# Hybrid gMLP and SSD block on one core: a hand-written order from the last wide pair to the second projection, PSUM banks from a queue, and operands of the second projection made beside the first

## The chip, the cores and the metric

The kernel runs on one core of one Trainium2 chip. Its time is the device time of one execution in microseconds (us); several executions are timed and the median counts. The profile comes from one further execution, whose own time is given beside its span. All data are fp32. A core has a matrix engine (TensorE, PE in the profile, with its weight loads as PEld), a vector engine (VectorE, DVE), a scalar engine (ScalarE, ACT), GpSimd (POOL), and a SyncE (SP) that only issues DMAs here. TensorE writes its sums into PSUM, eight banks of 128 x 512 fp32.

## The reference, cut to what matters

One layer with sequence 1024 and model width 1024, followed by a norm:

```python
h = rms_norm(x, norm_w) * (1 + scale) + shift          # scale, shift, gate from c @ ada_w
gm_u, gm_v, gm_z, ssm_z, xbc, dt_raw, g_a, g_b = split(h @ w_in)
y_a = spatial_gating(gelu(gm_u), gelu(gm_v), ...) * silu(gm_z)
xbc = silu(causal_depthwise_conv(xbc, conv_w, conv_b))
xs, bm, cm = split(xbc);  dt = softplus(dt_raw + dt_bias)
y_b = ssd_scan(xs, dt, -exp(a_log), bm, cm) + xs * d_skip   # 32 heads, 8 groups, chunks of 128
y_b = grouped_rms_norm(y_b * silu(ssm_z), ssm_norm_w)       # 2048 wide
merged = sigmoid(g_a) * (y_a @ w_proj_a) + sigmoid(g_b) * (y_b @ w_proj_b)
return rms_norm(x + gate * (merged @ w_out), final_norm_w)
```

## The kernel before, in words

**Products.** Each fp32 operand is split into a high part in fp32r (a rounded copy) and a low part (the operand less its high part), and a product is three matmuls: high by high, high by low, low by high. The three large products use a Strassen scheme with seven block products p1 to p7. Splitting one operand is two instructions: a cast for the high part (on ACT) and a subtraction for the low part (on DVE).

**Stages, in order.**
1. The input projection, in "pairs" of 128 columns (`pair`, `product` L567 to L573). Each of a pair's seven products takes twelve 128x512 matmuls. The last pair is called g14: it makes gate columns, and its sums c1 and c2 go through tanh (L906) and are stored to `th_d`. It runs its products as p1, p5, p6, p3, p7, p2, p4 and calls `beside(n)` (L1240) after each of the first five sums is copied out.
2. The SSD scan, in 32 steps (8 groups by 4 double chunks, listed in `order`, L1155). For each step, `decay_rows` and `decay_exps` make exponentials (ea, dcy) on ACT, with a mask on POOL between; `prep_products` makes transposes and products of B and C into banks px and pc, and weights them on DVE (dcy, xd); `prep_b` and `prep_xe` copy the rest out (bn, xe). `front` then makes yi and the state product sp; `back` makes yn and the step's output. The order of these is written by hand in the loop at L1388 to L1409.
3. Between the steps the first projection, `y_a @ w_proj_a`, is drawn as filler (`proj_a`, L1312, called through `draw`): 192 draws of two matmuls. It runs over eight column blocks dd; each has two PSUM banks pma and, per block, a high and a low part of the weights (wah, wal), made after the second and the fourth k step of the block before. When a block is complete, DVE multiplies its banks with a gate (tha, L1337), and the result is stored to `mt_d`. Its other operands, ya, are loaded in `beside` and split in `ya_operand` (L1208).
4. The second projection, `y_b @ w_proj_b`, in 56 units: seven products p1, p2, p5, p3, p6, p7, p4 by eight k steps, each unit with twelve matmuls into four banks (`multiply`, L1520). p1, p6, p7 and p4 use the four x banks, p2, p5 and p3 the four y banks. `loads(u)` (L1473) issues the DMAs of a unit, six units ahead; `operands(u)` (L1487) normalizes yn with the row factors rb (L1466), and makes high and low parts (bh, bl at L1505 and L1506; a at L1510 and L1511), four units ahead. After p1 ACT copies the x banks out as c11, and after p2 DVE adds the y banks to it (L1637). Later units make the gated sum (`merged`, L1559 to L1565).
5. The output projection and the last norm.

**What sets the order.** Engines run their instructions in order. A scheduler decides that order from modelled times and priorities, except for instructions that are pinned to program order: all matmuls of these stages, all loads on SP, and whatever goes through `keep` or `pin`. While `hand[0]` is true, every instruction of DVE, ACT and POOL is pinned. It is true only from the first `front` to the end of the SSD steps; the lines of instructions issued in that time show as L56. Stage 4 comes after that: its operands run at the scheduler's choice, but for the first four units, whose high and low parts are pinned.

**Memory.** PSUM banks of the SSD steps come from one ring (`bank`, tag "bk", eight buffers): a new tile waits until the tile eight before it is done. The banks of stage 4 are other tags ("bx0" and so on) in a new pool, which lie on banks that the old tiles held. SBUF slots of 128x512 come from a list `room`, with rings (`ring`, `turn`) for operands that rotate: rb has four slots, bh and bl five each.

Of the kernel before, what the change touches and what calls it, by code (L numbers as in the profile page):

```python
# [35 lines left out]
def hybrid_kernel(  # L36
# [105 lines left out]
    hp = hpool.__enter__()  # L142
    BN = ("b11", "t1", "t2", "b22", "t3", "b21", "t4")
# [337 lines left out]

    def bank(name):

        return psum.tile([P, 512], F32, name=name, tag="bk", bufs=n_banks[0])
# [90 lines left out]
    pending, n_banks = [], [6]  # L575
# [370 lines left out]
    class Group:  # L946
# [72 lines left out]
        def prep_b(self, s):  # L1019
            self.bn[s] = bn = p2x.tile([P, 256], F32, name=f"bn{self.g}_{s}", tag="bn", bufs=3)  # L1020
            A.copy(bn, self.raw[s][1][:, 256:512])  # L1021

        def prep_xe(self, s):
            self.xs[s].append(self.weighted(s, "xe", dde))

# [13 lines left out]
        def front(self, s):  # L1039

            g, nm = self.g, f"{self.g}_{s}"
            sl, dcy, ea = self.pre[s]
            bn, (xd, xe) = self.bn[s], self.xs[s]
            yi = bank(f"yi{nm}")
            for i in range(2):
                for h in range(HPG):
                    j, hh = h // 2, h % 2
                    mm(yi[hh * HD : (hh + 1) * HD, j * 256 + i * P : j * 256 + (i + 1) * P],
                       xd[:, i * 256 + h * HD : i * 256 + (h + 1) * HD], dcy[:, h, i, :])
            sp = bank(f"sp{nm}")  # L1050
# [16 lines left out]
            if not last:  # L1067
                self.nxt = self.state(f"st{nm}_1"), sp
                self.decayed(self.nxt[0], s, 1)

        def back(self, s):
# [16 lines left out]
            G.tensor_add(y1[:, :, t0:], y1[:, :, t0:], m[:, :, t0:])  # L1088
            if self.nxt is not None:
                self.st, sp = self.nxt  # L1090
                V.tensor_add(self.st, self.st, sp[:, 256:512])
                self.nxt = self.state(f"st{nm}_2")
                self.decayed(self.nxt, s + 1, 0)
# [4 lines left out]
        def post(self, q):  # L1098

            g = self.g  # L1100
            yz = self.yz[q]

            def leave():
                for j in range(2):
                    store(yb_d[2 * g + j][:, q * 512 : (q + 1) * 512], yz[:, j])

            if g < NG - 2 or q == 0:
                later(3, leave)
                later(9, self.squares, yz, [yz[:, j] for j in range(2)])
                later(17, self.post2, q, yz[:, 0])  # L1110
            else:
                later(1, leave)
                sq = [turn(r, f"sq{g}", F32) for r in (y1_r, ym_r)]
                later(1, self.squares, yz, sq, pin)
                later(9, self.post2, q, sq[0])
# [13 lines left out]
        def post2b(self, q, pq):  # L1129
            g = self.g  # L1130
            V.tensor_scalar(ssq[:, g * NCH + q * 4 : g * NCH + q * 4 + 4], pq[:, 0:4], 1.0 / 256, EPS,
                            op0=ALU.mult, op1=ALU.add)
            if q == 1:
# [5 lines left out]
        def post3(self, at_once=False):  # L1139
# [5 lines left out]
            V.tensor_copy(row, pr[0:NCH, 0:P])  # L1145
            to = rs_d[g].rearrange("o (c p) -> (o c) p", p=P)
# [61 lines left out]
    def ya_operand(k):  # L1208
        yh, yl = ya_raw[k]
        for i in range(2):  # L1210
            pin(A.copy(yh[i], f32(yl[i])))
# [13 lines left out]
    def wa_block(dd):  # L1225
        wa_high(dd)
        wa_low(dd)

    def wa_high(dd):
        was[dd] = []  # L1230
        for i, wr in enumerate(war[dd]):
            wh, wl = turn(wah_r[0], f"wah{dd}_{i}"), turn(wal_r[0], f"wal{dd}_{i}")
            A.copy(wh, wr)
# [6 lines left out]
    def beside(n):  # L1240

        if n == 0:
            ya_load(0)
            ya_load(1)
        elif n == 1:
# [16 lines left out]
    held, seconds, fold = [], [], []  # L1262
# [7 lines left out]
    for n, (name, _, _, d1, d2, g) in enumerate(todo):  # L1270
# [32 lines left out]
        if n + 1 == len(todo):  # L1303
            pair(name, ops, lambda t: held.append((d1, t)), lambda t: held.append((d2, t)), beside, True)
# [7 lines left out]
    def proj_a():  # L1312

        for dd in range(KT):
# [20 lines left out]
            keep = pin if dd == KT - 1 else lambda i: i  # L1335
            for h in range(2):
                keep(V.scalar_tensor_tensor(ths[h], ths[h], 1.0, pms[h], op0=ALU.add, op1=ALU.mult))  # L1337
            for h in range(2):
                to = mt_d[dd][:, h * 512 : (h + 1) * 512]
                if hand[0]:  # L1340
                    later(1, store, to, ths[h])
                else:
                    keep(A.dma_start(to, ths[h]))
# [44 lines left out]
    hand[0] = True  # L1388
# [21 lines left out]
    while tasks:  # L1410
        draw(2)
        run_tasks()
    hand[0] = False

    room.extend(ea_r[0] + [st_tag])
    room.extend(tag for k in range(KT - 2) for tag in ya_tags[k])
    draw(left[0] - 5)

    def banks(name, c):
        return [psb.tile([P, 512], F32, name=f"{name}{j}", tag=f"b{c}{j}") for j in range(4)]  # L1420
# [30 lines left out]
    first, rest = room[:3], room[10:21]  # L1451
    del room[10:21], room[:3]
    rb_r, bh_r, bl_r = (([first[n]] + [rest.pop(0) for _ in range(c)], [0]) for n, c in enumerate((3, 4, 4)))
# [127 lines left out]
    room.extend(tag for k in (KT - 2, KT - 1) for tag in ya_tags[k])  # L1581
    for tags, _ in (war_r[0], wah_r[0], wal_r[0], tha_r, y1_r, ym_r):
# [3 lines left out]
    psb = ps3.__enter__()  # L1586
    wo, wor = {}, {}
# [14 lines left out]
    sums, more = [], []  # L1602
    for u, (nm, k) in enumerate(units):
# [10 lines left out]
        multiply(u, ps)  # L1614
        ahead(u)
# [11 lines left out]
        if k % 2 and more and nm not in ("p2", "p5"):  # L1627
            merged(*more.pop(0))
        if k == KT - 1:
            for j in range(4):  # L1630
                with tc.high_priority():
                    if nm == "p1":
                        t = slot_tile(f"c11_{j}")
                        A.copy(t, psx[j])
                        more.append((j, 0, t, f"c11_{j}"))
                    elif nm == "p2":
                        V.tensor_add(more[j][2], more[j][2], psy[j])  # L1637
                    elif nm in ("p5", "p3"):
# [131 lines left out]
```

## Time and profile before

| what | us |
|---|---|
| median of the runs | 1423.65 |
| lowest and highest of three | 1422.61, 1425.19 |
| profiled execution | 1426.2 |
| its span, first to last instruction | 1424.5 |

The mean granted clock of TensorE in the profiled execution is 0.996 of full speed. In the profile's rows, times are in us from the span's start. A timeline row gives the start, the duration (of the whole group where several instructions are joined, with x and their number), engine, line, operation and tiles, and in brackets the time in which the engine was idle before it, with the engine and the line that ended this idleness. A row of the waits gives the engine and what it waited for: total us, how often, and the longest. A row of the windows gives the busy time of each engine in a stretch, the granted clock of TensorE, the busy share of the DMA engines, and GB/s.

### The profile page before, as it was taken

The page shows a single profiled execution, that of the slowest core. Times are in us where ns is not written, and L with a number is a line of the kernel's source. Part 1 is how long each engine was busy: PE and PEld are TensorE (multiplying, and loading weights), DVE is VectorE, ACT ScalarE, POOL GpSimd, SP SyncE. Part 2 cuts the span into 40 slices and gives each one's busy share as a digit, 9 for nine tenths or more (in the row PEclk, how much of TensorE's full clock was granted, in tenths as well). Part 3 has the DMA queues.
Part 4 walks back from the last instruction along what each step waited for, and adds up shares of the span by engine and source line. Part 5 has one row for each costly group of instructions (what it writes and reads, how often), then busy time and mean ns, then how long its engine had stood idle before and what let it go on. Part 6 is the DMA issues. An engine that isn't in the chain of part 4 may idle for free.

```text
span 1424.5 us, 20475 instructions
## 1 busy us (share of the span) xinstructions
PE 1391.4 (98%) x7087; PEld 1152.5 (81%) x7087; DVE 1026.6 (72%) x1821; ACT 783.4 (55%) x1444; POOL 205.2 (14%) x190
## 2 busy tenths in 40 slices
PE   8999999999999999999999999989999989999997
PEld 7678888888888888888887788878888878787886
DVE  4686677776677888788778786377778866948443
ACT  5664575666566665545565554657667633334201
POOL 0000000000000000000010100027879840000000
PEclk9999999999999999999999999999999999999999
DMA  8552333333323687587686764688888767977331
GB/s 264 157 170 83 125 106 110 100 115 104 117 83 112 196 240 220 157 255 225 197 244 187 227 200 133 228 319 280 278 286 286 255 209 259 380 253 292 136 118 74
DMA packets 260524, 277.08 MB, mean 195 GB/s; under 512 B 13596, under 2 KB 210628, under 8 KB 260420
## 3 DMA queue, kind: packets, MB, share of 16 engines
q1 hardware_dynamic: 179396, 195.37, 43.3%
q10 hardware_dynamic: 81024, 80.40, 16.2%
q8 instruction: 56, 0.92, 0.3%
q14 instruction: 48, 0.39, 0.1%
HBM read 191.40 MB, written 84.31 MB: 194 GB/s over the span
## 4 chain that ended last, share of the span: by engine, by line
PE 80%; DMA 6%; DVE 4%; ACT 3%; issue 3%; POOL 3%; SPq 1%; POOLq 0%; ACTq 0%; DVEq 0%
PE xx L571 6%; PE xuz L571 6%; PE xcb L571 6%; PE po L90 6%; PE xz L571 6%; PE x L1527 6%; PE xg L571 3%; PE pma L90 3%; PE yuz L571 3%; PE yx L571 3%; PE yp L1527 3%; PE xv L571 3%; PE ycb L571 3%; PE yz L571 3%; PE yv L571 2%
## 5 line engine op out<-in xcount | busy, mean ns | idle before, releaser
L782 POOL TENSOR_TENSOR wog<-wog,gb 128x1024 f32<-128x1024 f32 x8 | 22.6, 2825 | 725.5 <-ACT wbb L799 530.3
L56 ACT ACTIVATE dcy<-dcy,nacs 128x128 f32<-128x128 f32 x224 | 68.6, 388 | 32.6 <-POOL dcy L56 13.6
L90 PE MATMUL pma<-yh,wah 128*128 128x512 f32 x128 | 43.4, 419 | 1.8 <-ACT bn L1021 1.8
L894 ACT ACTIVATE ac<-ac 128x1024 f32<-128x1024 f32 x32 | 34.0, 1061 | 19.7 <-DVE ac L892 19.6
L1733 ACT ACTIVATE xr<-r 128x1024 f32<-128x1024 f32 x7 | 7.4, 1061 | 66.1 <-issue 39.0
L90 PE MATMUL pma<-yh,wal 128*128 128x512 f32 x128 | 42.8, 415 | 0.0
L56 DVE TENSOR_TENSOR ym<-yn,ea 128x512 f32<-128x512 f32 (+1 forms) x32 | 19.9, 623 | 30.5 <-PE yn L90 30.3
L56 POOL TENSOR_TENSOR yz<-y,sl 128x512 f32<-128x512 f32 x32 | 41.1, 1285 | 0.6
L90 PE MATMUL pma<-yl,wah 128*128 128x512 f32 x128 | 39.9, 393 | 0.0
L90 PE MATMUL yi<-dcy,xd 128*64 128x128 f32 x512 | 35.9, 283 | 3.5 <-DVE xe L1015 2.5
L56 POOL TENSOR_TENSOR y<-y,ym 128x512 f32<-128x512 f32 (+1 forms) x32 | 36.6, 1143 | 17.1 <-DVE ym L56 16.5
L1723 POOL TENSOR_TENSOR r<-r,fnw 128x256 f32<-128x256 f32 (+1 forms) x3 | 2.7, 915 | 247.9 <-ACT xr L1722 247.9
L892 DVE SCALAR_TENSOR_TENSOR ac<-c2x,cwt,ac 128x1023 f32<-128x1023 f32 (+2 forms) x24 | 31.9, 1330 | 9.0 <-ACT ac L890 7.1
L56 DVE TENSOR_TENSOR dcy<-dcy,pc 128x1024 f32<-128x1024 f32 x30 | 36.6, 1219 | 2.4 <-PE pc L93 1.4
L1732 DVE TENSOR_TENSOR r<-po,xr 128x1024 f32<-128x1024 f32 x7 | 8.6, 1225 | 39.8 <-PE po L90 39.7
L1466 DVE SCALAR_TENSOR_TENSOR yn<-yn,par,rb 128x512 f32<-128x512 f32 x32 | 24.9, 779 | 15.7 <-DMA yn<-yb_d 15.7
L56 ACT ACTIVATE ea<-dcy 64x512 f32<-64x512 f32 x56 | 35.3, 630 | 1.5 <-DMA dcy<-acs_d 1.1
L892 DVE SCALAR_TENSOR_TENSOR ac<-c2cb,cwt,ac 128x1023 f32<-128x1023 f32 (+2 forms) x24 | 30.6, 1276 | 7.1 <-ACT ac L890 7.0
L56 POOL TENSOR_SCALAR_AFFINE_SELECT dcy<-dcy 128x1024 f32<-128x1024 f32 x28 | 32.2, 1152 | 19.7 <-ACT ea L56 19.6
L90 PEld LDWEIGHTS yi<-dcy,xd 128*64 128x64 f32 x512 | 28.1, 139 | 7.8 <-issue 5.5
L90 PE MATMUL sp<-xe,bn 128*128 128x256 f32 x112 | 33.4, 415 | 0.0
L56 DVE SCALAR_TENSOR_TENSOR y<-sl,dskt,yi 128x256 f32<-128x256 f32 x64 | 27.7, 473 | 6.3 <-PE yi L90 2.8
(2844 smaller groups left out, 4425.8 us busy)
## 6 DMA issues: line engine op xcount, KB each, us to landing
sl<-s_d SPq DMA_DIRECT2D x32, 768.0 KB
s_d<-ac ACTq DMA_DIRECT2D x32, 512.0 KB
dcy<-acs_d SPq DMA_DIRECT2D x32, 512.0 KB
aw<-in_ada_w_dram SPq DMA_DIRECT2D x16, 512.0 KB
wbr<-in_w_proj_b_dram SPq DMA_DIRECT2D x64, 128.0 KB
wb_d<-wbb ACTq DMA_DIRECT2D x32, 256.0 KB
wb_d<-wbc ACTq DMA_DIRECT2D x32, 256.0 KB
yb_d<-yz ACTq DMA_DIRECT2D x32, 256.0 KB
```

The lines of the kernel that those rows point to most:

```text
L56: return lambda *a, **k: tc.keep_in_program_order(f(*a, **k))
L90: pin(PE.matmul(acc, l, r, start=first, stop=last))
L571: pin(PE.matmul(ps, lw[:, k * P : (k + 1) * P], r[k], start=first and n + k == 0, stop=n == 2 and k == 3, skip_group_check=not first))
L782: G.tensor_mul(w, w, gb)
L892: V.scalar_tensor_tensor(ac[:, s:], cc[:, : S - s], conv_wt[:, 3 - s, i : i + 1], ac[:, s:], op0=ALU.mult, op1=ALU.add)
L894: A.activation(ac, ac, AF.Silu)
L1466: V.scalar_tensor_tensor(t, t, snw[:, n : n + 1], rbs[n // 2, h], op0=ALU.mult, op1=ALU.mult)
L1527: pin(PE.matmul(ps[j], a[:, v, js], r, start=first and n + k == 0, stop=n == 2 and k == KT - 1, skip_group_check=not first))
L1723: G.tensor_mul(r[:, cs], r[:, cs], fnw[:, cs])
L1732: V.tensor_add(r, pw, xr)
L1733: A.activation(xr, r, AF.Square, accum_out=sq[:, 0:1])
```

## The change

- **Order.** `hand[0]` becomes true before the last pair and stays true until the end of p5 (unit 23), so that in this stretch DVE, ACT and POOL run in program order.
- **Last pair.** `beside` now also issues `decay_rows` and `decay_exps` of the first two SSD steps and, after p6's copy, the first two ya operands and the first weight block, with their high parts on DVE (four ya and two wah copies). The other ya operands follow later. The two steps' `prep` and the pair's own last tanh and store come in program order around p2 and p4, where before these were held back or scheduled.
- **PSUM.** A queue `free` holds the numbers of the eight banks, at first in the order 1, 4, 3, 0, 2, 7, 5, 6. A new tile takes the bank at the head of the queue; `release` puts a bank at the end of it behind the instruction that reads it last. The x banks of stage 4 are the first four of the queue at the end of the SSD steps, the y banks the last four.
- **First operands of stage 4.** The first loads and operands are issued in the loop that draws the last filler, at fixed draws, not after it. Each unit's parts (norm, bh, bl, a) follow one another. Rings for these now use slots of the SSD steps: rb three, bh and bl four each. ya slots are handed back one by one as the last block of the first projection consumes them.
- **p1 to p5.** c11's copies and additions are issued directly after p1's and p2's last unit, ahead of the next unit's operands. The last block's store goes through `store`.

The diff, cut to its core:

```diff
+    free, at_bank = [], {}
     def bank(name):
-        return psum.tile([P, 512], F32, name=name, tag="bk", bufs=n_banks[0])
+        if not free and not at_bank:
+            return psum.tile([P, 512], F32, name=name, tag="bk", bufs=6)
+        at_bank[name] = free.pop(0)
+        return psum.tile([P, 512], F32, name=name, tag=f"k{at_bank[name]}")
+    def release(*names):
+        free.extend(at_bank.pop(name) for name in names if name in at_bank)
...
     def start_ssd():
         fetch(2)
-        for n in range(2):
-            later(3 + 5 * n, decays, n + 1)
-            g, s = order[n]
-            later(13 + n, groups[g].prep, s)
+        done_d[0] = 2
...
     def beside(n):
+        first = [(groups[g], i) for g, i in order[:2]]
         if n == 0:
             ya_load(0)
             ya_load(1)
+            first[0][0].decay_rows(first[0][1])
         elif n == 1:
...
+            first[1][0].decay_rows(first[1][1])
+            first[0][0].decay_exps(first[0][1])
         elif n < 5:
             ya_load(2 * n - 2)
             ya_load(2 * n - 1)
-        if n == 4:
-            for k in range(2):
-                ya_operand(k)
-            wa_block(0)
-            for k in range(2, 6):
-                ya_operand(k)
+        if n == 2:
+            ya_operand(0, V.tensor_copy)
+            first[1][0].decay_exps(first[1][1])
+            ya_operand(1, V.tensor_copy)
+            wa_high(0, V.tensor_copy)
+            wa_low(0)
+        elif n == 4:
+            ya_operand(2)
+            ya_operand(3)
+        elif n > 4:
+            first[n - 5][0].prep(first[n - 5][1])
+            ya_operand(n - 1)
...
-            pair(name, ops, lambda t: held.append((d1, t)), lambda t: held.append((d2, t)), beside, True)
+            hand[0] = True
+            pair(name, ops, with_last(5, d1), with_last(6, d2), beside, True)
...
             for h in range(2):
-                keep(V.scalar_tensor_tensor(ths[h], ths[h], 1.0, pms[h], op0=ALU.add, op1=ALU.mult))
+                V.scalar_tensor_tensor(ths[h], ths[h], 1.0, pms[h], op0=ALU.add, op1=ALU.mult)
+                release(f"pma{dd}_{h}")
...
-    n_banks[0] = 8
+    numbered(psum, "k")
+    free.extend(BANKS)
     for k in (6, 7):
         ya_operand(k)
-    decays(3)
-    for f, t in held:
-        f(t)
     decays(4)
...
-    while tasks:
-        draw(2)
-        run_tasks()
-    hand[0] = False
...
-    rb_r, bh_r, bl_r = (([first[n]] + [rest.pop(0) for _ in range(c)], [0]) for n, c in enumerate((3, 4, 4)))
+    rb_r = ea_r[0], [0]
+    bh_r, bl_r = ((r[0][0][:2] + ya_tags[0][2 * n : 2 * n + 2], [0]) for n, r in enumerate((wah_r, wal_r)))
...
-    for u in range(LOAD):
-        loads(u)
-        if u > 1:
-            operands(u - 2)
+    for u in range(3):
+        loads(u)
+    n = 0
+    while tasks:
+        draw(2)
+        run_tasks()
+        ya_free()
+        n += 1
+        if n in (2, 4, 6, 8):
+            operands(n // 2 - 1)
+        if n in (4, 5, 6):
+            loads(n - 1)
     draw(left[0] + 1)
...
+    places_of = {"x": free[:4], "y": free[4:]}
...
+    def emptied_banks(nm):
+        for j in range(4):
+            if nm == "p1":
+                t = slot_tile(f"c11_{j}")
+                A.copy(t, psx[j])
+                more.append((j, 0, t, f"c11_{j}"))
+            else:
+                V.tensor_add(more[j][2], more[j][2], psy[j])
...
         multiply(u, ps)
+        if u < 16 and k == KT - 1:
+            emptied_banks(nm)
         ahead(u)
...
+        if u == 23:
+            hand[0] = False
```

More of the change, by code (lines that the diff above doesn't have):

```diff
@@ L1066, in front @@
             self.nxt = None
-            if not last:
+            release(f"yi{nm}")
+            if last:
+                release(f"sp{nm}")
+            else:
                 self.nxt = self.state(f"st{nm}_1"), sp
@@ L1206, in ya_load, with ya_operand @@
         ya_raw[k] = yh, yl
-    def ya_operand(k):
+    def ya_operand(k, copy=None):
         yh, yl = ya_raw[k]
         for i in range(2):
-            pin(A.copy(yh[i], f32(yl[i])))
+            pin((copy or A.copy)(yh[i], f32(yl[i])))
             pin(V.tensor_sub(yl[i], f32(yl[i]), f32(yh[i])))
@@ L1386, in of @@
         getattr(groups[g], f)(s)
-    hand[0] = True
     draw(6)
@@ L1574, in ahead, with ya_free @@
             operands(u + LEAD)
-    for u in range(LOAD):
-        loads(u)
-        if u > 1:
-            operands(u - 2)
+    emptied = [1]
+    def ya_free():
+        while emptied[0] < KT and left[0] <= 3 * (KT - 1 - emptied[0]):
+            room.extend(ya_tags[emptied[0]])
+            emptied[0] += 1
+    for u in range(3):
+        loads(u)
+    n = 0
[8 more added lines that the diff above has]
+            loads(n - 1)
     draw(left[0] + 1)
-    room.extend(tag for k in (KT - 2, KT - 1) for tag in ya_tags[k])
-    for tags, _ in (war_r[0], wah_r[0], wal_r[0], tha_r, y1_r, ym_r):
+    ya_free()
+    for tags in (war_r[0][0][:2], wah_r[0][0][2:], wal_r[0][0][2:], tha_r[0], y1_r[0], ym_r[0]):
         room.extend(tags)
@@ L1626, in hybrid_kernel @@
             wo_parts(next(iter(wor)))
-        if k % 2 and more and nm not in ("p2", "p5"):
+        if k % 2 and more and u > 23:
             merged(*more.pop(0))
-        if k == KT - 1:
+        if u == 23:
+            hand[0] = False
+        if u > 15 and k == KT - 1:
             for j in range(4):
                 with tc.high_priority():
[L1632 to L1638, printed above, removed]
+                    if nm in ("p5", "p3"):
                         t = slot_tile(f"{nm}_{j}")
```

43 lines of the change are left out of this document (26 added, 17 removed).

## The prediction

> **What bounds the kernel now.** I read the page's first part, then the windows by 50 us, then the waits of PE, then the timeline around the longest of them.
>
> ```profile
> span 1424.5 us, 20475 instructions
> PE 1391.4 (98%) x7087; PEld 1152.5 (81%) x7087; DVE 1026.6 (72%) x1821; ACT 783.4 (55%) x1444; POOL 205.2 (14%) x190
> ```
>
> TensorE is busy for 98% of the span. The change adds and removes no matmul, and on PE the order of instructions stays exactly what it was; POOL's too. So the only time it can win is PE's idle time, and PE's slow time, between the last wide pair (from about 905 us) and p5 (to about 1240 us). It can lose what new waits cost there.
>
> ```profile
> core 0: us, PE busy (x) PEld busy (x) DVE busy (x) ACT busy (x) POOL busy (x), PEclk, DMA share, GB/s
> 900.00:950.00 50.00, 45.70 (x226) 37.24 (x225) 27.80 (x45) 35.98 (x77) 5.89 (x6) 0.97 0.84 298
> 1150.00:1200.00 50.00, 45.57 (x212) 37.34 (x212) 32.16 (x55) 19.05 (x35) 8.76 (x6) 0.97 0.73 247
> 1200.00:1250.00 50.00, 47.78 (x210) 38.94 (x209) 47.69 (x78) 16.56 (x28) 0.00 (x0) 1.00 0.97 368
> ```
>
> All three windows fall short, two of them at a granted clock of 0.97. In the third, DVE is busy for 47.69 of 50 us and the DMA engines for 0.97: there the change has little room on other engines. The waits of PE from 890 to 1300 us, summed by releaser, name the places:
>
> ```profile
> PE x L1527 <- DVE tha L1337: 3.5, 1, 3.5
> PE yi L90 <- DVE xe L1015: 2.5, 1, 2.5
> PE pma L90 <- ACT bn L1021: 1.8, 1, 1.8
> PE yn L90 <- POOL st_home L56: 1.4, 2, 0.8
> PE yp L1527 <- ACT p5bh L1505: 1.3, 1, 1.3
> PE yn L90 <- DVE st_home L56: 1.3, 2, 0.9
> PE yp L1527 <- DVE c L1637: 0.9, 1, 0.9
> ```
>
> Each row: total, times, longest. Rows two and three are the start of the SSD steps, row one the start of p1, the L1527 rows with yp the start of p5; the rest are small waits inside the SSD steps, whose order was already written by hand.
>
> **The change part by part.**
>
> *A, start of the SSD steps.* Timeline rows, in order of engine (start, length, idle before and its releaser):
>
> ```profile
> 932.90 0.50 PE L90 MATMUL pma<-yh,wah 128*128 128x512 f32 x1 [1.75 <-ACT bn L1021]
> 933.24 0.63 PE L90 MATMUL pma<-yl,wah 128*128 128x512 f32 x2
> 938.23 1.97 PE L90 MATMUL yi<-dcy,xd 128*64 128x128 f32 x16 [2.53 <-DVE xe L1015]
> 940.13 1.75 PE L90 MATMUL sp<-xe,bn 128*128 128x256 f32 x4
> 941.53 0.81 PE L90 MATMUL pma<-yh,wah 128*128 128x512 f32 x2
> 946.36 1.09 PE L90 MATMUL yi<-dcy,xd 128*64 128x128 f32 x16
> 947.38 1.13 PE L90 MATMUL sp<-xe,bn 128*128 128x256 f32 x4
> 948.16 0.81 PE L90 MATMUL pma<-yl,wah 128*128 128x512 f32 x2
> 930.02 0.58 ACT L587 COPY c2g<-xg 128x512 f32<-128x512 f32 x1
> 930.49 1.14 ACT L1211 CAST yh<-yl 128x512 fp32r<-128x512 f32 x2
> 933.79 1.28 ACT L978 ACTIVATE ea<-dcy 64x512 f32<-64x512 f32 x2
> 943.71 1.12 ACT L56 CAST wah<-wa 128x512 fp32r<-128x512 f32 x2
> 920.33 0.69 DVE L587 TENSOR_TENSOR c1g<-c1g,yg 128x512 f32<-128x512 f32 x1 [12.38 <-PE yg L571]
> ```
>
> The first projection's bank waits 1.75 us for the copy of bn, because a fixed ring hands it the bank that pc holds; the queue hands it the bank freed longest ago, so this wait goes. The first step's yi waits 2.53 us for xe, which on DVE stands behind the ya operands; the preparation now goes ahead of them, and six high-part copies (four ya, two wa, each 1.14 / 2 = 0.57 us on ACT) move to DVE, into its idle 12.38 us before 920. That cover exists whatever the ACT does; without it they would cost 6 x 0.57 = 3.4 us of DVE before c1g. After the second wait the same 16 + 4 matmuls need 941.53 - 938.23 = 3.30 us, against 948.16 - 946.36 = 1.80 in the next step: 1.5 us of slow clock. **Removed: 1.75 + 2.53 + 1.5 = 5.8 us.**
>
> After a gap of 2.53 us the clock fell; after the one of 1.75 it did not (933.24 shows two matmuls at 0.63). The Trainium skill, "TensorE: Matmul & The Clock Gate", "Part 1: The HAM clock gate", has the clock halved after an idle window of about 3.4 us, and that window free-running; the fall after 2.53 us here speaks against the length. By the page's length the 1.5 us would not belong to the gap and would stay, the gain being 1.5 us less; I go by the row.
>
> What is late next: ACT's own line. In program order the pair's last tanh, its store, bn and six more casts now stand ahead of the third step's ea. From 930.02: copy 0.58, tanh about 1.1, issue and bn about 0.7, six casts 3.4: 935.8, against 933.79 before, and up to 937 if the store waits for a landing. From ea to the second projection block's wah the distance was 943.71 - 933.79 = 9.9 us, so wah comes at 945.7 and its second half ends at 946.8, while PE, 5.8 us less 0.2 sooner, asks for it at about 945.7. I take a stall of 0.5 us (to 2.0). On DVE the wal parts, which wait for wah, now stand in line ahead of the second step's y, the state and the two tha products that empty the first projection banks: these end near 949.4, and pc of the next step but one, queued for such a bank, asks at 947.5: 1.9 us more. **New stalls: 2.4 us, bounds 0 and 5.8.** Net of A: 3.4.
>
> *SSD steps.* They keep their orders. The few bank waits that move from px to pc move by at most 0.2 us; the small waits (1.4, 1.3) stay. Cost 0, bounds -1 and +2.
>
> *B, start of p1.*
>
> ```profile
> 1166.84 0.39 PE L1527 MATMUL x<-p1bh,p1a 128*128 128x512 f32 x1
> 1172.49 0.50 PE L1527 MATMUL x<-p1bh,p1a 128*128 128x512 f32 x1 [3.45 <-DVE tha L1337]
> 1173.06 0.65 PE L1527 MATMUL x<-p1bh,p1a 128*128 128x512 f32 x2
> 1177.17 0.40 PE L1527 MATMUL x<-p1bl,p1a 128*128 128x512 f32 x1
> 1177.40 0.62 PE L1527 MATMUL x<-p1bh,p1a 128*128 128x512 f32 x2
> 1177.86 0.39 PE L1527 MATMUL x<-p1bl,p1a 128*128 128x512 f32 x1
> 1163.68 0.62 ACT L1505 CAST p1bh<-yn 128x512 fp32r<-128x512 f32 x1 [3.33 <-DVE yn L1466]
> 1164.33 0.69 DVE L1506 TENSOR_TENSOR p1bl<-yn,p1bh 128x512 fp32r<-128x512 f32 x1 [0.92 <-ACT p1bh L1505]
> 1164.94 0.75 DVE L1466 SCALAR_TENSOR_TENSOR yn<-yn,par,rb 128x512 f32<-128x512 f32 x1
> ```
>
> Two x banks were those of the last pma, freed by the last tha products, which the scheduler had put behind operand parts of p1. In the changed kernel the x banks are the four freed first; two wait only for the ssq of two earlier groups, short instructions. The 3.45 us go. After them, 11 matmuls took 1177.17 - 1173.06 = 4.11 us, against 11 x 0.23 (two in 1177.86 - 1177.40) = 2.53: 1.6 us of slow clock. **Removed: 5.0 us.** Next late: the operands, now strictly one unit after the other on DVE: yn 0.66, wait for ACT's cast 0.6, low part 0.6, low part of the weights 0.6: 2.5 to 2.7 us a unit, where PE takes 12 x 0.23 = 2.76 us. The first starts at about 1163 and PE at 1166.8, so even with the two tha (2 x 0.6) in between the fifth unit's operands keep 0.7 to 1.2 us of slack. I cost this at 0 if loads come in time, and at 1.0 us in all for one that does not (bounds 0 and 16, below). SP's loads for the last tha move behind eight loads of p1; they are needed only when the last pma is complete, right before 1166.84, and by then they hold up no PE bank: cost 0.
>
> *C, start of p5.*
>
> ```profile
> 1217.50 0.47 PE L1527 MATMUL yp<-p5bh,p5a 128*128 128x512 f32 x1 [1.34 <-ACT p5bh L1505]
> 1219.31 0.50 PE L1527 MATMUL yp<-p5bh,p5a 128*128 128x512 f32 x1 [0.88 <-DVE c L1637]
> 1216.72 0.68 DVE L1637 TENSOR_TENSOR c<-c,yp 128x512 f32<-128x512 f32 x1
> 1218.58 1.87 DVE L1637 TENSOR_TENSOR c<-c,yp 128x512 f32<-128x512 f32 x3
> ```
>
> The wait put down to p5bh is the bank's: the add that empties it ran at 1216.72, among other parts, and the next three after 1218.58. The changed order has the four adds directly after p2's last unit, ahead of the fourth p5 unit's parts. Each of a unit's four banks takes three matmuls, 0.69 us: bank j is complete 2.07 - 0.69 j us before p2 ends and wanted 0.69 j after it; at 1.87 / 3 = 0.62 us an add, all four are in time. **Removed: 1.34 + 0.88 = 2.2 us**, bounds 0 and 2.2.
>
> *Sum:* 5.8 + 5.0 + 2.2 = 13.0 removed, 2.4 + 1.0 new: 9.6 us gained. Against the profiled execution, 1426.2 us (span 1424.5 and 1.7 around it), that is 1416.6; the execution lay 2.55 us above the median 1423.65, so I forecast **1414.0 us**.
>
> The Trainium skill, "SBUF — State Buffer", "Who interferes with whom", says that a copy on VectorE can hold a port that GpSimd needs, fully blocking it; the six moved copies are such. No run here shows it; by it POOL's masks beside them would start some tenths later, far from PE.
>
> **Rivals.**
>
> *The waits move to the operands.* In p1, DVE waits in line for a norm whose load is late. For: this row, 15.7 us of such waits in before.
>
> ```profile
> L1466 DVE SCALAR_TENSOR_TENSOR yn<-yn,par,rb 128x512 f32<-128x512 f32 x32 | 24.9, 779 | 15.7 <-DMA yn<-yb_d 15.7
> ```
>
> Against: they fell where DVE was ahead. If B's gain is lost whole, 1414.0 + 5.0 = 1419.
>
> *The SSD start gives all back* (ea at 937, a second gap with slow clock behind it): A nets 0, 1417.4.
>
> *The transfers give it back.* At 0.97 of the DMA time in 1200 to 1250, p5 and p3 cannot come forward by more than some 1.5 us per 50; of B and C's 6.2 net, 4.7 is lost: 1418.7. Against: the loads are issued six units (16 us) ahead, and the window before has a share of 0.73.
>
> *Slower.* The ring of rb is three tiles instead of four, bh and bl four instead of five. SP stands in line at each rb load until the norm of five units earlier, and everything behind it waits too. This decides if a load takes longer from issue than about five units (13.6 us) less the DVE's delay. Then each of the eight pairs of p5 and p3 units comes late by about 2 us: 16 us, 1414 + 16 = 1430.
>
> *The change does not do it:* banks still conflict elsewhere; within 0.2% of 1423.65.
>
> **How the numbers follow.** Forecast (1409.5 to 1417) 0.53; operands 0.12 (1419); transfers 0.08; SSD start 0.05; no change 0.09; slower 0.13. A measurement of this kernel can tell about 0.2% (2.8 us) from no change. Faster: 0.53 + 0.12 + 0.08 + 0.05 = 0.78, less 0.03 for the rivals' upper ends; same 0.12; slower 0.13. The low end is all 13.0 removed and 1 more in the SSD steps: 1409.5. The high end takes in all but the slower rival: 1424.5.
>
> **What would show it.** Right: no idle row at the pma after bn, at the first yi, at the fourth x matmul group, nor at p5; granted clock 1.00 in the 50 us around p1; one gap of some 2 us near pc about 947 us. Wrong: PE waits on p1bl or p1a, on yn through DVE, or DVE idle over 3 us before yn in p1; a p5a or rb landing over 13 us after its issue.

## The result, and the profile after

The changed kernel is slower: median 1434.68 us (1432.29 to 1435.68) against 1424.72 us for the kernel before on the same chips. The ratio is 1.0066, with a 95% interval of 1.0051 to 1.0081. The forecast was 1414.0 us with a range of 1409.5 to 1424.5. Its profiled execution has a span of 1433.4 us. The page's first part and the windows of the changed kernel, with the columns of those shown of before:

```profile
span 1433.4 us, 20485 instructions
PE 1394.2 (97%) x7087; PEld 1152.3 (80%) x7087; DVE 1030.4 (72%) x1827; ACT 781.1 (54%) x1438; POOL 205.7 (14%) x190
```
```profile
900.00:950.00 50.00, 48.28 (x248) 39.49 (x247) 32.95 (x54) 33.69 (x71) 6.00 (x6) 1.00 0.84 289
1150.00:1200.00 50.00, 48.07 (x223) 39.07 (x222) 31.00 (x53) 20.13 (x36) 5.35 (x4) 1.00 0.81 263
1200.00:1250.00 50.00, 41.14 (x166) 32.87 (x165) 43.70 (x70) 14.15 (x24) 0.00 (x0) 0.93 0.92 339
1250.00:1300.00 50.00, 47.22 (x198) 37.96 (x198) 27.87 (x46) 15.93 (x27) 0.00 (x0) 0.97 0.61 201
```

At the start of the SSD steps and in p1 things came as forecast: PE is busy for 48 of 50 us in the first two windows (before 45.7 and 45.6), at a clock of 1.00. Then PE falls to 41.1 of 50, at a clock of 0.93, though DVE is less busy than before (43.7 against 47.7). An engine that is less busy while its consumer starves is waiting itself. (DVE waits in p1, p2 and p5, but not in p3, as is told below.) The waits of PE (total us, times, longest) in the changed kernel, from the last pair to the start of the output projection:

```profile
PE yp L1548 <- DVE p3bl L56: 6.7, 3, 4.3
PE yp L1548 <- issue: 4.4, 1, 4.4
PE yp L1548 <- DVE tri L56: 1.9, 1, 1.9
PE pc L90 <- DVE tha L56: 1.7, 1, 1.7
PE po L90 <- DVE tg L1580: 2.2, 1, 2.2
```

The waits for bn, for the first xe and for tha at p1 are gone. New are 1.9 us at the start of p2, 4.4 at the start of p5, 6.7 in p3, and 2.2 at the start of the output projection. Behind the gaps at p5 and in p3 the clock fell; behind the 1.9 and 2.2 us it did not (1.00 from 1180 to 1200 and from 1335 to 1350). Three stretches of 10 us (1210, 1240 and 1250) show a clock of 0.83. By an estimate of 0.17 x 10 that cost 1.7 us each, 5.1 together:

```profile
1210.00:1220.00 10.00, 7.63 (x27) 6.21 (x28) 8.28 (x14) 2.35 (x4) 0.00 (x0) 0.83 1.01 381
1240.00:1250.00 10.00, 5.67 (x18) 4.25 (x18) 10.00 (x18) 2.11 (x4) 0.00 (x0) 0.83 0.58 235
1250.00:1260.00 10.00, 7.83 (x27) 6.02 (x27) 9.07 (x16) 1.24 (x2) 0.00 (x0) 0.83 0.32 93
```

How far ahead of the kernel before is each kernel when a step begins? The table takes each step's first matmul, in us from the span's start in the profiled executions, less the same in the kernel before (negative is sooner; the experiments are told below). Its first column is the addition of c2 in the last pair, at 922.98 before, ahead of any gain of the change:

| kernel | last pair | p1 | p2 | p5 | p3 | p6 | first po | last po |
|---|---|---|---|---|---|---|---|---|
| changed | +0.2 | -5.2 | -10.4 | -5.1 | -4.8 | +5.9 | +6.4 | +8.9 |
| e1, scheduler's operands | -1.0 | -5.9 | -10.5 | -6.0 | -4.6 | -4.6 | -4.3 | -3.0 |
| e2, norm ahead | +0.5 | -2.8 | -8.2 | -9.5 | -10.6 | -9.2 | -9.1 | -7.8 |
| e3, larger rings | -2.0 | -4.7 | -10.1 | -6.7 | -5.6 | +5.7 | +6.4 | +7.2 |
| e4, before with strict order | -1.0 | -1.3 | +2.4 | +2.8 | +1.7 | +10.0 | +9.9 | +10.0 |
| e5, output banks | -2.1 | -6.6 | -12.0 | -12.7 | -13.9 | -12.3 | -12.3 | -12.2 |
| e10, rows early | -0.8 | -6.1 | -11.5 | -13.0 | -14.3 | -13.6 | -13.4 | -13.4 |

The changed kernel is 10.4 us ahead when p2 begins, and 5.9 behind when p6 begins: **16.3 us are lost inside p2, p5 and p3**, 10.7 of them in p3. The rows above nearly add up to it: waits of 1.9 + 4.4 + 6.7, slow clock of about 5.1, less the 2.2 us that the kernel before waits at p5, are 15.9. Already in the last pair the traces lie up to 2.7 us apart (e2 and e5), so single numbers say less than the steps from one column to the next.

**The mechanism in p1, p2 and p5**, as the two timelines of the changed kernel show it. DVE in p2 (start, length, idle before and who ended it):

```profile
1193.69 0.69 DVE L56 TENSOR_TENSOR p2bl<-yn,p2bh 128x512 fp32r<-128x512 f32 x1 [0.76 <-ACT p2bh L56]
1194.30 0.69 DVE L56 TENSOR_TENSOR p2a<-p2r,p2a 128x512 fp32r<-128x512 f32 x1
1194.90 0.75 DVE L56 SCALAR_TENSOR_TENSOR yn<-yn,par,rb 128x512 f32<-128x512 f32 x1
1196.41 0.69 DVE L56 TENSOR_TENSOR p2bl<-yn,p2bh 128x512 fp32r<-128x512 f32 x1 [0.76 <-ACT p2bh L56]
```

and ACT beside it:

```profile
1195.76 0.62 ACT L56 CAST p2bh<-yn 128x512 fp32r<-128x512 f32 x1 [1.58 <-DVE yn L56]
1196.28 0.61 ACT L56 CAST p2a<-p2r 128x512 fp32r<-128x512 f32 x1
1198.47 0.62 ACT L56 CAST p2bh<-yn 128x512 fp32r<-128x512 f32 x1 [1.58 <-DVE yn L56]
```

In every unit DVE waits for ACT's cast, and ACT waits for DVE's next norm. Norm to cast 0.86, cast to low part 0.65, two low parts 0.61 and 0.60: 2.72 us from one p2bl to the next (1196.41 - 1193.69), which is just what PE needs for a unit. DVE cannot gain a lead, that is, run further ahead of PE than it was at the start. In p5 the line is longer, for each unit has a difference (2.84 us in the first three units), and from the fourth unit on the gate's parts stand in between:

```profile
1215.57 0.62 ACT L56 CAST p5bh<-yn 128x512 fp32r<-128x512 f32 x1 [4.62 <-DVE yn L56]
1218.89 0.62 ACT L56 CAST p5bh<-yn 128x512 fp32r<-128x512 f32 x1 [2.70 <-DVE yn L56]
1222.21 0.62 ACT L56 CAST p5bh<-yn 128x512 fp32r<-128x512 f32 x1 [2.18 <-DVE yn L56]
```

A cast every 3.32 us, 0.6 more than PE takes. The line also began with a small lead. DVE stood ready for its first low part for 8.1 us, but ACT's line was held by the stores of tha, which waited for a landing; the low part came 2.6 us ahead of p1's first matmul (1161.63), about as in the kernel before (2.5):

```profile
1155.80 2.50 ACTq L56 DMA_DIRECT2D mt_d<-tha  x2
1158.35 0.62 ACT L56 CAST p1bh<-yn 128x512 fp32r<-128x512 f32 x1 [3.23 <-DMA tha<-th_d]
1159.00 0.69 DVE L56 TENSOR_TENSOR p1bl<-yn,p1bh 128x512 fp32r<-128x512 f32 x1 [8.11 <-ACT p1bh L56]
```

In the kernel before, the scheduler put other units' norms into the time of the cast. DVE's waits for casts between 1150 and 1265 us, total, times and longest, first in the changed kernel and then before:

```profile
DVE p1bl L56 <- ACT p1bh L56: 13.4, 8, 8.1
DVE p2bl L56 <- ACT p2bh L56: 6.4, 8, 1.0
DVE p5bl L56 <- ACT p5bh L56: 4.9, 8, 0.8
```
```profile
DVE p1bl L1506 <- ACT p1bh L1505: 1.3, 2, 0.9
DVE p2bl L1506 <- ACT p2bh L1505: 0.3, 1, 0.3
```

The lead, from the start of a unit's low part to the unit's first matmul, was at p2's first unit 6.8 us before and 1.6 us in the changed kernel; at p3's first unit 9.1 and 2.8, at its second 8.1 and 0.2. Much of the old lead was PE's own lateness: it grew by 4.3 us in p1, where PE lost 5.0, and by 2.3 from p2 to p3, where PE waited 2.2. Taking PE's waits away took this lead away too.

Two waits for banks come from the same line. At the start of p2 the second y bank still held a norm row, and the short copy that empties it (tri) started only at 1186.28, behind two low parts: 1.9 us. At p5 the adds that empty the y banks come late. DVE's first add starts at 1211.59, right behind the third p5bl, 3.6 us after the end of p2's last matmul; the profile puts the 4.4 us down to "issue":

```profile
1210.98 0.69 DVE L56 TENSOR_TENSOR p5bl<-yn,p5bh 128x512 fp32r<-128x512 f32 x1 [0.76 <-ACT p5bh L56]
1211.59 2.48 DVE L56 TENSOR_TENSOR c<-c,yp 128x512 f32<-128x512 f32 x4
```
```profile
1212.37 0.76 PE L1548 MATMUL yp<-p5bh,p5a 128*128 128x512 f32 x1 [4.37 <-issue]
```

**p3 is another matter.** There DVE does not wait for ACT: it is busy for 10.00 of the 10 us from 1240 (the window above), as it is in the kernel before from 1220 to 1250. What PE waits for is the order of DVE's work at the seam where the strict order ends. Units 24 to 27, the first four of p3, are pinned (L56); the units behind them are the scheduler's (L1527). The low part of the third p3 unit could start when its cast ended, at 1240.27, but it started at 1245.61: a later unit's low part and eight more instructions, most of them differences for p6 and p7, stood ahead of it. The row of ACT is that cast, the last row is PE:

```profile
1239.65 0.63 ACT L56 CAST p3bh<-yn 128x512 fp32r<-128x512 f32 x1 [0.33 <-DVE yn L56]
1240.13 0.69 DVE L1527 TENSOR_TENSOR p3bl<-yn,p3bh 128x512 fp32r<-128x512 f32 x1
1245.61 0.69 DVE L56 TENSOR_TENSOR p3bl<-yn,p3bh 128x512 fp32r<-128x512 f32 x1
1246.35 0.80 PE L1548 MATMUL yp<-p3bl,p3a 128*128 128x512 f32 x1 [4.33 <-DVE p3bl L56]
```

The fourth unit's low part came at 1252.36 in the same way, behind another later one at 1249.95, and PE waited 2.2 us. With a longer lead part of this might have been covered; how much was not tried.

### The profile page after: what moved, and what is told of

Read it like the earlier page. It is cut to its first block, busy times and chain, and to the rows that moved or that the text cites. A ratio compares the mean times of both kernels' runs of the same rounds, so it can differ in the third digit from the quotient of the medians.

```text
span 1433.4 us, 20485 instructions
## 1 busy us (share of the span) xinstructions
PE 1394.2 (97%) x7087; PEld 1152.3 (80%) x7087; DVE 1030.4 (72%) x1827; ACT 781.1 (54%) x1438; POOL 205.7 (14%) x190
## 4 chain that ended last, share of the span: by engine, by line
PE 77%; DMA 7%; DVE 7%; ACT 3%; issue 2%; POOL 2%; SPq 1%; ACTq 0%; POOLq 0%; DVEq 0%
PE xuz L585 6%; PE xcb L585 6%; PE po L90 6%; PE xx L585 6%; PE xz L585 5%; PE xg L585 5%; PE pma L90 3%; PE yuz L585 3%; PE xv L585 3%; PE ycb L585 3%; PE yx L585 3%; PE yp L1548 3%; PE yz L585 3%; PE yg L585 2%; PE yi L90 2%
## 5 line engine op out<-in xcount | busy, mean ns | idle before, releaser
L56 ACT ACTIVATE dcy<-dcy,nacs 128x128 f32<-128x128 f32 x256 | 78.4, 389 | 34.4 <-POOL dcy L56 16.2
L56 POOL TENSOR_SCALAR_AFFINE_SELECT dcy<-dcy 128x1024 f32<-128x1024 f32 x32 | 37.4, 1169 | 106.0 <-ACT ea L56 105.9
L56 DVE TENSOR_TENSOR ym<-yn,ea 128x512 f32<-128x512 f32 (+1 forms) x32 | 19.9, 623 | 30.2 <-PE yn L90 30.0
L56 POOL TENSOR_TENSOR yz<-y,sl 128x512 f32<-128x512 f32 x32 | 41.2, 1287 | 0.6
L56 ACT ACTIVATE ea<-dcy 64x512 f32<-64x512 f32 x64 | 40.2, 629 | 1.8 <-DMA dcy<-acs_d 1.3
L56 DVE TENSOR_TENSOR dcy<-dcy,pc 128x1024 f32<-128x1024 f32 x32 | 39.0, 1219 | 2.6 <-PE pc L93 1.4
L56 POOL TENSOR_TENSOR y<-y,ym 128x512 f32<-128x512 f32 (+1 forms) x32 | 36.7, 1146 | 12.7 <-DVE ym L56 12.6
L1779 DVE TENSOR_TENSOR r<-po,xr 128x1024 f32<-128x1024 f32 x7 | 8.6, 1225 | 41.2 <-PE po L90 41.1
L906 DVE SCALAR_TENSOR_TENSOR ac<-c1cb,cwt,ac 128x1023 f32<-128x1023 f32 (+2 forms) x24 | 30.6, 1276 | 0.7 <-ACT ac L904 0.7
L906 DVE SCALAR_TENSOR_TENSOR ac<-c1x,cwt,ac 128x1023 f32<-128x1023 f32 (+2 forms) x24 | 30.6, 1277 | 0.0
```

The lines of the kernel that those rows point to most:

```text
L56: return lambda *a, **k: tc.keep_in_program_order(f(*a, **k))
L906: V.scalar_tensor_tensor(ac[:, s:], cc[:, : S - s], conv_wt[:, 3 - s, i : i + 1], ac[:, s:], op0=ALU.mult, op1=ALU.add)
L1779: V.tensor_add(r, pw, xr)
```

## The experiments

Theory 1: the strict order of one unit after the other makes DVE and ACT alternate. Theory 2, the rival that the prediction gave for a slower kernel: the smaller rings keep SP's loads in line.

**e1: the scheduler places the operand parts again.**

```diff
     def operands(u):
+        was_hand, hand[0] = hand[0], False
+        operands_of(u)
+        hand[0] = was_hand
+
+    def operands_of(u):
...
```

> The changed kernel, but the scheduler again chooses where the operand parts of the second projection stand on VectorE and ScalarE (only the first four units' parts stay pinned); everything else as changed. Theory 1 (the strict order makes VectorE wait for ScalarE's cast in every unit and ScalarE for VectorE's norm, so that a unit takes 2.72 us in p2 and 2.84 to 3.32 us in p5 against 2.72 us on TensorE, and no lead is ever built): the idle 2.0, 4.5, 4.5 and 2.3 us of TensorE at p2, p5 and p3 go with the slow clock behind them; p6 starts some 10 us sooner than in the kernel before; 1414 to 1419 us. Theory 2 (the smaller rings and SP waiting in line for them): no change, 1431 to 1436 us.

Measured: 1424.55 us, ratio to before 0.9997 (0.9987 to 1.0008). Some 10 us come back, p3's waits are gone (no unit is pinned against others, so there is no seam), and p6 begins 4.6 us sooner than before. Theory 2 cannot explain that, since the rings are the changed ones. But the time misses theory 1's 1414 to 1419: at p2 and p5 waits remain.

```profile
PE yp L1553 <- issue: 3.4, 1, 3.4
PE yp L1553 <- DVE p2bl L1532: 1.0, 1, 1.0
PE yp L1553 <- ACT p2bh L1531: 0.7, 1, 0.7
```

The scheduler's order is not good by itself: it works from modelled times, and DVE waits for late yn loads 12.5 us in all here (1140 to 1265 us; about as much, 15.7, in the kernel before).

**e2: order by hand, but the next norm between casts and low parts.**

```diff
...
         keep(A.copy(hi, t))
+        if nm not in WB:
+            a, raw = aops[u], raws.pop(u)
+            keep(A.copy(a[:, 0], raw))
+        if 0 < u < 23:
+            normed(u + 1)
         keep(V.tensor_sub(lo, t, f32(hi)))
...
```

`normed` is y_norm, and in p5 the difference, of the next unit; it is made once.

> The changed kernel with its order still fixed by hand, but the norm of the next unit (and in p5 the difference) stands between a unit's two casts and its two low parts, so that VectorE has work while ScalarE casts. Rings and banks as changed. Theory 1: a unit takes VectorE some 1.9 to 2.0 us in p1 and p2 instead of 2.72, a lead builds, and the stalls at p5 and p3 go: 1414 to 1420 us. Theory 2 (rings): no change, 1431 to 1436 us.

Measured: 1418.86 us, ratio 0.9955 (0.994 to 0.997). The stretch stays ordered by hand, rings and banks are the changed ones, and in each unit only the place of the norm (in p5 with its difference) differs; instead of losing 16.3 us from p2 to p6 it gains 1.0 (-8.2 to -9.2). DVE in p2 of e2:

```profile
1192.63 0.68 DVE L56 TENSOR_TENSOR p2bl<-yn,p2bh 128x512 fp32r<-128x512 f32 x1
1193.24 0.68 DVE L56 TENSOR_TENSOR p2a<-p2r,p2a 128x512 fp32r<-128x512 f32 x1
1193.90 0.75 DVE L56 SCALAR_TENSOR_TENSOR yn<-yn,par,rb 128x512 f32<-128x512 f32 x1
1194.57 0.69 DVE L56 TENSOR_TENSOR p2bl<-yn,p2bh 128x512 fp32r<-128x512 f32 x1
```

1.94 us from one p2bl to the next (1194.57 - 1192.63), with no wait for ACT, where it was 2.72. Not every unit runs so: DVE waits here for late yn loads, 6.0 us in all from 1140 to 1265, and p2's eight low parts are 2.65 us apart on the mean. The lead was won in p1: it is 5.6 us at p2's first unit (1.6 in the changed kernel) and 6.2 at p3's first (2.8). Theory 1 holds for p1, p2 and p5. For p3 e2 does not decide, for a second thing differs there: in its trace all four pinned low parts (1223.71, 1227.39, 1231.06, 1236.66) stand ahead of the first later one (1237.26), and PE waits 1.1 us.

**e3: the ring sizes of before, strict order kept.**

```diff
-    rb_r = ea_r[0], [0]
+    rb_r = ea_r[0] + [ya_tags[1][0]], [0]
```

and one more slot each for bh and bl.

> The changed kernel with the ring sizes of the kernel before: rb four slots instead of three, bh and bl five instead of four; the strict order stays. Theory 1: the period of 2.72 us and the stalls at p5 and p3 stay, 1432 to 1436 us. Theory 2 (rings): they go or halve, 1415 to 1427 us.

Measured: 1433.41 us, ratio 1.0061 (1.0046 to 1.0076), with p3's and p5's waits about as they were:

```profile
PE yp L1548 <- DVE p3bl L56: 7.2, 3, 4.9
PE yp L1548 <- issue: 4.4, 1, 4.4
```

Theory 2 falls.

**e4: the kernel before, with the strict order alone.**

```diff
-                if hand[0]:
+                if dd < KT - 1:
                     later(1, store, to, ths[h])
                 else:
-                    keep(A.dma_start(to, ths[h]))
+                    store(to, ths[h])
...
         run_tasks()
-    hand[0] = False
...
+        if u == 23:
+            hand[0] = False
```

> The kernel before with one part of the change alone: program order stays on from the SSD steps to the third step's end (unit 23) instead of ending with the SSD steps; banks, rings, and the place of the first operands as before. Theory 1: the same alternation of VectorE and ScalarE, so p5 and p3 wait as in the changed kernel, 1429 to 1440 us. If the loss needs another part of the change (rings, banks): 1422 to 1427 us.

(The first part keeps the last block's store where it was, at once.) Measured: 1437.53 us, ratio 1.009 (1.0075 to 1.0105). The strict order alone makes the kernel before about as slow as the whole change does, or slower. Here DVE starts p2 with a lead of 9.9 us, for PE itself was held up in p1 (the 6.4 us below); in p5 the period is the same 3.32 us, and at p3's first unit 3.9 us are left. The loss is in p3, 8.3 us (+1.7 to +10.0), at the same seam: a later unit's low part at 1248.86 stands ahead of the third pinned one at 1250.67, and PE waits for the third and the fourth:

```profile
PE x L1526 <- DVE tha L56: 6.4, 1, 6.4
PE yp L1526 <- DVE p3bl L56: 5.2, 2, 3.4
```

The wait for tha at p1 grew from 3.5 to 6.4 us, where tha stands in the same strict line; that the line alone made it longer was not tried by itself.

**e5 to e8: what e2 leaves.** e5 moves the first output products off three of the four x banks, to banks 4 to 7, by taking four other tiles first; at the end of the SSD steps the queue stood at 1, 7, 2, 3, 0, 4, 5, 6, so that x had taken three of the four banks that the first output products use.

```diff
+    free[:2] = free[1::-1]
     places_of = {"x": free[:4], "y": free[4:]}
...
+    for h in range(4):
+        one(f"one{h}")
```

> As e2, but the first output products lie on banks 4 to 7 instead of 0 to 3, and the x banks are taken in the order 7, 1, 2, 3, so that only one of these four banks is an x bank and its last reader comes first. If the bank queue (which put x on 1, 7, 2, 3, under the first output products) is what makes the output projection start late, the wait of po for the gate (1.0 us in e2, 2.2 us in the changed kernel) goes and the way from the first po to the last shortens from 88.8 to about 87.5 us as in the kernel before: 1417 to 1418 us. If something else delays po: as e2, 1418.9.

Measured: 1415.73 us, ratio 0.9948 (0.993 to 0.9966). The wait of po is gone, and from the first po matmul to the last it takes 87.5 us, as before (88.8 in e2, 90.0 in the changed kernel). So the bank queue caused the 2.2 us. (e5 is 3.1 us faster than e2 by the medians; 1.3 of it lie in this stretch, and e5's trace was 2.7 us sooner already in the last pair.)

e6 puts the cast of the second weight block first:

```diff
-                if k == 1 and dd + 1 < KT:
+                if k == 1 and 0 < dd < KT - 1:
                     wa_high(dd + 1)
...
+    wa_high(1)
     decays(4)
     fill = proj_a()
```

> As e2, but the high part of the second weight block of the first projection stands on ScalarE ahead of the fourth step's exponentials, not behind them. If that cast is what VectorE's line (wal, y, tha) and so pc's bank wait for, the wait of 1.6 to 2.1 us at pc near 949 us goes: 1416.5 to 1417.5 us. If another wait (the store's landing, tha's load) ends last there: as e2, 1418.9.

Measured: 1418.84 us, as e2 (ratio to before 0.996, 0.9946 to 0.9973). The cast came early, and pc waited longer, 2.5 us, because the gate's load ended last:

```profile
948.62 1.35 DVE L56 SCALAR_TENSOR_TENSOR tha<-tha,pma 128x512 f32<-128x512 f32 x2 [3.45 <-DMA tha<-th_d]
```

e7 puts the squares of the last two groups ahead of the stores:

```diff
-                later(1, leave)
...
                 later(1, self.squares, yz, sq, pin)
+                later(1, leave)
```

> As e2, but in the last two groups ScalarE's squares stand ahead of the stores of the same data, whose issue waits for earlier transfers. If the stores hold up ScalarE's line, TensorE's wait for the squares (1.4 us in e2) goes, and VectorE's wait of 8.9 us for the first cast of p1 shrinks by 3 us or more: 1417 to 1418 us. If the later store of tha holds up the line anyway: the 8.9 us stay, 1418 to 1419.

Measured: 1418.33 us (ratio 0.9957, 0.9936 to 0.9979). The wait for the squares went, but the first cast of p1 still came 7.9 us after DVE wanted it: the store of tha holds ACT's line, as the second case had it.

e8 has the edits of e5, e6 and e7 together.

> The edits of e5, e6 and e7 together on e2. If the three waits are independent, 1.2 + 2.0 + 1.4 us come off: about 1414 to 1415 us. If the loads of p2 and p5, which depend on the last groups' norms, cannot come sooner, the gain of the early parts returns as waits in p2 or p3: 1416 to 1418.

Measured: 1416.48 us (0.9948, 0.993 to 0.9966), no better than e5 alone.

**e9 to e12.** e9 is e5 with each block's tha loads ahead of the weight loads:

```diff
-            if dd + 2 < KT:
-                wa_load(dd + 2)
             ths, pms = [], []
...
                 pms.append(bank(f"pma{dd}_{h}"))
+            if dd + 2 < KT:
+                wa_load(dd + 2)
```

> As e5, but in each block of the first projection the two loads of the gate tha are issued ahead of the weight loads of two blocks later, not behind them. If the landing of tha (948.6 us in e6 although the cast was early) is what the bank of pc waits for, the wait of 1.6 us there goes: about 1414 us. If VectorE's line after the late cast is as late as the landing, only some tenths go: 1415 to 1416.

Measured: 1417.21 us (0.9945, 0.9927 to 0.9964), as e5. Now tha waits for no load, and starts just as late, behind wal and y in DVE's line; pc waits 1.4 us.

```profile
948.22 1.28 DVE L56 SCALAR_TENSOR_TENSOR tha<-tha,pma 128x512 f32<-128x512 f32 x2
948.95 0.49 PE L90 MATMUL pc<-sl 128*128 128x128 f32 x2 [1.40 <-DVE tha L56]
```

e10 is e9 with the norm rows of the last two groups one unit sooner (`k in (3, 4)` for `k in (4, 5)`).

> As e9, but the norm rows of the last two groups are made at the fourth and fifth unit of p1, not at the fifth and sixth. SP's line then stands 2.7 us less at the load of these rows, and all loads behind come sooner. If late loads cause what is left at p5 and p3 (0.9 and 1.4 us), 1 to 2 us come off e9: about 1412.5 us. If the alternation left in p3 (whose first units are not prepared ahead) causes them: as e9.

Measured: 1414.73 us, ratio 0.9931 (0.9912 to 0.995), the lowest median of all, though its interval and e9's overlap. The row of the seventh group left at 1175.30 instead of 1179.73 in e9 (p1 began 1.6 us sooner, too), SP's next load of rb could go at 1180.40 instead of 1183.25, and the waits at p5 (0.5 us in e9) and p3 (1.6) shrink to none and 0.4.

e11 has the same edit on e1.

> As e1 (the scheduler places the operand parts), with the same rows one unit sooner. In e1 SP stands in line until 1183.8 us for the row of the seventh group, and p2 and p5 then wait 2.1 and 3.6 us. If that line is why e1 gained less than e2, those waits shrink by 2 to 4 us together: 1419 to 1422 us. If the scheduler's order is the reason by itself: 1423 to 1426 us.

Measured: 1425.47 us (1.0004, 0.9992 to 1.0016), no gain. The row left only 0.4 us sooner than in e1 (1182.17 against 1182.57), but in a trace whose p1 began 2.1 us later; counted from p1's start it left 2.5 us sooner, so the edit did what it was made for. PE's waits did not go: it waits 1.6 us for low parts in p1 and 3.7 at p2. The time lies where the expectation puts the scheduler's order as the reason by itself. What in that order gains less than e2 is not settled.

e12 is e10 with e6's cast.

> As e10 (norm ahead, output banks, gate tha loaded first, rows one unit sooner), and with the cast of e6: the second block's high weight part ahead of the fourth step's exponentials. Alone, neither the cast (e6) nor the load (e9) moved the wait of 1.4 to 2.5 us at pc. If the two end within some tenths of each other and pc waits for the later one, both together take 1 to 1.5 us off: about 1413 to 1414 us, with the gap at pc under 0.5 us. If a third thing ends last there: the gap stays, 1414.5 to 1415.5.

Measured: 1416.87 us, ratio 0.9927 (0.9909 to 0.9945). pc no longer waits for tha; 4 us later another pc waits 2.1 us for the state:

```profile
950.28 0.49 PE L90 MATMUL pc<-sl 128*128 128x128 f32 x2 [2.09 <-DVE st_home L56]
```

The third step's yi starts as in e9 (952.21 against 952.22), so nothing was won. Cast, load and state chain, it seems, were all about equally late, and removing one or two of three shows nothing; the state chain itself was not made sooner in any run.

## Why the prediction was wrong, point by point

- **A, the start of the SSD steps: right.** Net 3.4 us were forecast. The third step's yi starts at 952.68 instead of 956.56 us, 3.9 sooner. The new gap was forecast as 1.9 us ending at 949.4; it is 1.65 us and ends at 949.41, at the instruction named; the 0.5 us forecast for wah did not come (PE has no wait for it). The cover for the six moved copies held, though barely: before c1g VectorE is idle for 0.16 us where it was 12.38.

```profile
949.41 0.49 PE L90 MATMUL pc<-sl 128*128 128x128 f32 x2 [1.65 <-DVE tha L56]
952.68 1.09 PE L90 MATMUL yi<-dcy,xd 128*64 128x128 f32 x16 [0.35 <-DMA tha<-th_d]
```

Of its cause only a part was seen: e6, e9 and e12 show the landing of tha and VectorE's line level with each other.

- **B, the start of p1: right for p1, and not carried on.** The wait and its slow clock went: from p1 to p2 the changed kernel gains 5.2 us (5.0 forecast). "2.5 to 2.7 us a unit, where PE takes 12 x 0.23 = 2.76 us" was close too (2.72), and in p1 PE waits for no operand, as costed. The step that failed is that this cost, 0 and 1.0 us for a late load, stood for the whole strict stretch, though it was worked out for p1 alone: p2, p5 and p3 were put at nothing. A line as slow as its consumer builds no lead, and p5 and p3 need one. The runs showed waits of 1.9 us at p2 and 6.7 in p3 in its place. "Four units ahead" is where the code asks for the operands, not where they are.
- **C, the start of p5: wrong.** "All four adds are in time" took VectorE to be free when p2 ends. In program order the adds stand behind three p5 units' parts, each with its wait for ACT. In place of 2.2 us gained came a wait of 4.4.
- **p5 and p3: not worked out at all.** The sum of one p5 unit in strict order, norm, difference, wait, low part and a share of the gate, is 3.32 us by the same rows that gave 2.7 for p1; the lead falls from 7.1 us at p5's first unit, where PE was held by the bank, to 2.8 at p3's first. In p3 VectorE is busy for 10.00 of the 10 us from 1240 in both kernels, as the prediction's own window (47.69 of 50 us) hinted, and the end of the strict order put later units' parts ahead of the pinned ones. Of the 16.3 us, 10.7 are lost there, with the slow clock behind the waits. That the strict order is the cause, e1 and e4 show; how the loss in p3 divides between the missing lead and the seam, no run shows, for e1 and e2 changed both.
- **The output projection: not seen.** The forecast followed the queue to the x banks at p1 and no further. Whose banks come next cost 2.2 us.
- **The rivals.** "The waits move to the operands" named the place for p1, with loads as the cause, and priced it at 5 us; it came in p2, p5 and p3, with the order as the cause. The slower rival priced p5 and p3 at 16 us, near the 16.3 measured, but by rings, which e3 rules out; the nearness is luck. The transfers did not hold PE back: in e2 it passes the stretch from p2 to p6 1.0 us faster than before, at a DMA share of 1.03 from 1190 to 1215 us.

## What to carry to other kernels

When an order is written by hand over two engines that feed each other, write down the time around the loop for one unit, waits included, and compare it with the consumer's time for that unit; put an independent instruction of the next unit between every hand-over and its use. A lead is a stock: find where it is built, what starts the line, and which stage spends it. Where an order by hand ends, look at the seam: what a scheduler places freely can end up ahead of what was fixed. And follow a queue of buffers to its last user, not just to the one whose wait it was made to remove.

## What the runs showed of the hardware that was not expected

The slow clock does not need a gap of one certain length. In these traces a 10 us window fell to 0.83 behind idle times of PE of 1.9 us (pc near 950 us in e2), and 2.5 us (e6); it stayed at 1.00 behind 1.65, 1.9 and 2.2 us (changed kernel, at pc, p2 and po) and also behind 2.1 us (e12):

```profile
950.00:960.00 10.00, 9.92 (x60) 8.88 (x61) 7.87 (x15) 5.95 (x16) 6.65 (x8) 0.83 0.96 308
```
```profile
950.00:960.00 10.00, 8.11 (x51) 6.47 (x51) 6.66 (x12) 8.72 (x25) 8.13 (x10) 1.00 0.77 255
```

The first row is e2, the second e12. The Trainium skill ("TensorE: Matmul & The Clock Gate", "Part 1: The HAM clock gate") calls its window of about 3.4 us free-running; that the same idle time has either outcome agrees with it, while falls behind 1.9 us are shorter than the idle window it names. A gap of about 2 us thus costs 2 us or, by the estimate of 1.7 us above, 3.7; what decides between the two no trace here shows.

VectorE's instructions took longer beside GpSimd's masks, where the prediction had the masks a few tenths late. In the changed kernel the cast of yh at 913.34 took 1.32 us beside a mask that ran from 912.84 to 914.37, and the low part at 914.75 took 1.63 beside the other mask; the other three such casts took 0.41 to 0.43, and the other three low parts 0.69. That is 1.8 us of the cover before c1g, and TensorE lost nothing by it. That the masks caused it is inferred from the overlap.
